# Priority of the blocks and sums of h, the place of a weight sum, and the queue place of the third HGRN pair, in a one-core hybrid encoder block

## The chip, the cores and the metric

The kernel runs on one core of one Trainium2 chip. The time is the device time of one execution in microseconds (us). The kernel before took 1408.69 us as the median of three runs (1408.69, 1410.4, 1408.69).

Five engines work beside each other, each through its own instructions in order: TensorE (PE: matmuls, PEld: weight loads), VectorE (DVE), ScalarE (ACT), GpSimd (POOL) and SyncE (SP), which here only issues loads. They wait for each other and for DMA transfers by semaphores.

## The reference

One layer of a streaming encoder for 256 tokens of width 2048, all in float32: a normed input projection, an HGRN2 recurrence with 8 heads beside a chunked attention with 16 heads, a gated merge, and a squared-ReLU MLP.

```python
def mixer_block(u, w_in, lb, hg_norm_w, rel_bias, w_branch_a, w_branch_b, w_out):
    z = u @ w_in
    hq, hf, hi, hg, aq, ak, av, gates = jnp.split(z, SPLIT_POINTS, axis=-1)
    g = lb + (1.0 - lb) * jax.nn.sigmoid(hf)
    log_g, kk = jnp.log(g), 1.0 - g
    q = jax.nn.silu(hq) * (HG_DK ** -0.5)
    o = hgrn2_scan(q, kk, hi, log_g)          # per head, S_t = diag(g_t) S_{t-1} + k_t v_t^T, o_t = S_t^T q_t
    y_a = rms_norm(o, hg_norm_w) * jax.nn.silu(hg)
    y_b = chunk_band_attention(aq, ak, av, rel_bias)
    gate_a, gate_b = jnp.split(jax.nn.sigmoid(gates), 2, axis=-1)
    merged = gate_a * (y_a @ w_branch_a) + gate_b * (y_b @ w_branch_b)
    return merged @ w_out

def reference(x, ...):
    h = x + mixer_block(rms_norm(x, norm_mix_w), ...)
    h = h + jnp.square(jax.nn.relu(rms_norm(h, norm_mlp_w) @ w_up)) @ w_down
    return rms_norm(h, norm_final_w)
```

## The kernel before

**Matmuls by split halves.** Each float32 weight tile is loaded raw (`raw`, `rawp`, `rawd`; 128x1024 elements, 512 KB), cast on ACT to a high half (`wh`, line L89) and subtracted on DVE to a low half (`wl`, L90). The activations are held as the same kind of pair (`act_x`, `act_h`, `act_m`, `S_h`). A product of a 128-row block takes three matmuls per k-tile: hi by wh (L143), hi by wl (L144), lo by wh (L145). So each weight tile of 1024 columns costs one ACT cast, one DVE subtraction and 12 matmuls of 128x512.

**Stages in order.** The projections hf and hq (transposed, `gemm_t`, L184 to L188) and hi and hg (`gemm`) with the HGRN work between them; the attention's aq, ak, av and its scores; the gates ga and gb; the branch products ba and bb; w_out (units wo0 and wo2); then four quarters of w_up (units up00, up02, up10, ...) and w_down (dn...). From the gates on, all but the branch products are `Unit`s run by `run`.

**The queue of the HGRN stage.** `later` puts (gap, function) turns into one list, `behind`. Each weight tile of a projection calls `tick` (1 per k-tile of `gemm_t`, 2 per k-tile of `gemm`), which counts the first turn's gap down and runs it when it is used up. So the small HGRN matmuls and their DVE and ACT work come between the projection's matmuls. For a pair of heads `fq(u)` gives two functions: `decay` (`hf_pair`: sigmoid, gate, `kk` L319, floor L320, Ln L322, cumulative sum L324) and `query` (`hq_pair`: factor L330, sigmoid L332, products L335 and L338). `scores` queues eight turns for a pair (diagonal ps L373, factors L384 to L406, level matmuls L417, `so` L451). `group` queues, for two pairs, four outputs (`po` matmuls L475 and L476, square L480, sum L481, `o` L486) and four finishes (`tpo` transposes L493 and their split into `act_ya`). Pairs 0 and 1 make group 0, pairs 2 and 3 group 1. `a2[1]()` and `a2[2]()` are decay and query of the third pair; in the kernel before they are called at once, while group 0's turns are still in the list.

**A unit.** `run` computes a 256x1024 piece by a Strassen-like scheme of seven products over blocks of activation sums (`S_x`, `S_m`, `S_h`: lines L680 to L686, `combos`) and of weight sums (`sums`, L817, on DVE; `sent`, L822, an accumulating DMA from POOL). Its weight blocks are A, B, C and D, each two raw tiles; p11A in a name is the weight split for product 11 with block A. Items `r1_8`, `r0_14`, ... are plain weight tiles for the k-tiles that the scheme leaves. The last plain tiles of a unit (`r1_12`, `r1_14`) are done inside the next unit, from the list `late`.

**What sets the order.** A scheduler places each instruction on its engine; priority is the program's order, moved forward by `tc.high_priority(offset=2000)`. Weight splits, weight sums and evictions of banks are so marked. The transposes of h (`tp_h`, L106), its blocks (L1013, split L89 and L90, square L1015) and its sums come as `steps` of units wo2 and up00 (`h_blocks`): h is the residual after w_out, and up00 is the first unit that reads it. Loads are issued by SP in program order when their buffer is free; the stores of h to DRAM (`hd`) and the accumulating copies go through POOL's queue.

Of the kernel before, what the change touches and what calls it, by code (L numbers as in the profile page):

```python
# [12 lines left out]
ALU = mybir.AluOpType  # L13
# [3 lines left out]
P = 128  # L17
T = 256
NM = T // P
# [17 lines left out]
def bc(ap, pos, n):  # L37

    dims = [list(d) for d in ap.ap]
    dims.insert(pos, [0, n])  # L40
    return bass.AP(tensor=ap.tensor, offset=ap.offset, ap=dims)
# [9 lines left out]
def tile_hybrid_block(  # L51
# [5 lines left out]
    nc = tc.nc  # L57
# [13 lines left out]
    wmix, wmlp = vt[:, 0:16], vt[:, 16:32]  # L71
# [16 lines left out]
    def split(hi, lo, src, copy=None):  # L88
        (copy or nc.scalar.copy)(hi, src)  # L89
        nc.vector.tensor_tensor(lo, src, hi.bitcast(F32), op=ALU.subtract)  # L90
# [68 lines left out]
    def later(*steps):  # L159
        behind.extend([n, f] for n, f in steps)  # L160
# [57 lines left out]
    for kt, n in zip(starts, steps):  # L218
# [3 lines left out]
        with tc.high_priority(offset=2000):  # L222
            for j in range(n):
                g, hi = wmix[:, kt + j:kt + j + 1], xT[c][:, a + j, 0, :]
# [116 lines left out]
    def v_chunk(g):  # L341
        acc = gemm(xT, w_in_n, C_HI + g * NC, KD, f"hi{g}")
        vs = []
        for m in range(NM):
            v = hp.tile([P, NC], F32, name=f"v{g}{m}", tag="tok", bufs=7)
            nc.scalar.activation(v, acc[:, m, :], AF.Copy, scale=rstd[:, m:m + 1])
            vs.append(v)
        return vs
# [168 lines left out]
    def scores(n, made, gap, first=None, between=()):  # L517

        sc = []
        steps = []  # L520

        def one(i):
            if not i:
                out, fs = hgrn_scores(n, made)
                sc.extend(out)
                steps.extend(fs)
            steps[i]()

        todo = [(gap if i or first is None else first, lambda i=i: one(i)) for i in range(8)]
        for at, f in between:  # L530
            todo.insert(at, (gap, f))
        later(*todo)
        return sc

    def group(g, s0, s1, vs, gws, gap, gap2):
        parts = {}

        def outputs(h0, sc, m):
            if not m:
                parts[h0] = hgrn_out(g, h0, sc, vs, gws)  # L540
            parts[h0][0][m]()

        later(*[(gap, lambda h0=h0, sc=sc, m=m: outputs(h0, sc, m)) for h0, sc in ((0, s0), (2, s1)) for m in range(NM)],
              *[(gap2, lambda h0=h0, m=m: parts[h0][1][m]()) for h0 in (0, 2) for m in range(NM)])

    ya += [new_act(f"ya{g}") for g in range(2)]
    a0, a1 = fq(0), fq(1)
# [2 lines left out]
    s0 = scores(0, a0[0], 5, 12, ((5, a1[1]), (8, a1[2])))  # L550
    vs0 = v_chunk(0)
    s1 = scores(1, a1[0], 4)
    gws0 = hg_chunk(0)
    group(0, s0, s1, vs0, gws0, 4, 3)
    a2 = fq(2)
    a2[1]()
    a2[2]()
    s2 = scores(2, a2[0], 4)
    a3 = fq(3)
    later((3, a3[1]), (3, a3[2]))  # L560
    vs1 = v_chunk(1)
    s3 = scores(3, a3[0], 4)
    gws1 = hg_chunk(1)
    group(1, s2, s3, vs1, gws1, 2, 3)
    acc_q = [gemm_t(xT, w_in_t, C_AQ + i * T, KD, f"aq0{i}") for i in range(2)]
    while behind:
        tick(9)
# [91 lines left out]
    def combos(lhs, what, home, made, blocks=None):  # L659

        a = {}

        def block(m, j):
            if blocks:
                a[m, j] = blocks[m, j]
                return
            a[m, j] = fours(token(f"a{m}{j}_{what}"))
            x = lhs[j][:, :, :, m * P:(m + 1) * P].bitcast(F32)
            nc.vector.tensor_tensor(a[m, j], x[:, :, 0, :], x[:, :, 1, :], op=ALU.add)

        def final(i, s):
            t = home.tile([P, 4, 2, P], F32R, name=f"S{i}_{what}", tag=f"S{i}", bufs=1)
            split(t[:, :, 0, :], t[:, :, 1, :], s)
            made[i] = [[t[:, k, u, :] for u in range(2)] for k in range(4)]

        def one():
            for m in range(NM):
                for j in range(2):
                    block(m, j)
            nc.vector.tensor_tensor(a[1, 1], a[1, 0], a[1, 1], op=ALU.subtract)  # L680
            final(5, a[1, 1])

        def two():
            nc.vector.tensor_tensor(a[1, 0], a[0, 0], a[1, 0], op=ALU.subtract)
            nc.vector.tensor_tensor(a[0, 0], a[1, 1], a[0, 0], op=ALU.subtract)
            nc.vector.tensor_tensor(a[0, 1], a[0, 1], a[0, 0], op=ALU.add)  # L686
            final(4, a[0, 1])

        return [one, two, lambda: final(2, a[0, 0]), lambda: final(7, a[1, 0])]
# [165 lines left out]
    def run(u, then=None):  # L855

        def q():
            if late:
                late.pop(0)()

        def item(x):
            if x and x.items:
                x.load_item()

        if not u.raw:
            u.load("A")
            u.load("B")
            u.load("C")
            u.load("D")
        for _ in range(3 - sum(type(k) is tuple for k in u.raw)):  # L870
            item(u)
        at = iter(range(99))
        u.bank("11")
        u.product("11", "A", u.block(0, 0), True)
        u.sums("A", "B")
        u.begun("21", "11")
        u.sent("B", "C")
        q()
        item(u)
        u.bank("22")  # L880
        u.product("22", "A", u.comb(5), True)
        u.sums("A", "C")
        u.begun("12", "22")
        q()
        item(u)
        u.steps = list(u.make_steps())
        u.step(next(at))
        u.product("12", "C", u.comb(4))
        u.step(next(at))
        u.product("11", "D", u.block(0, 1))  # L890
        u.sent("D", "A")
        u.step(next(at))
        u.plain(1, (8, 9))
        item(u)
        u.step(next(at))
        u.product("21", "A", u.comb(2))
        u1 = u.copy(token(f"u1_{u.what}"), "21")
        if then:
            then.load("A")
        u.step(next(at))  # L900
        u.plain(1, (10, 11))
        u.less("12", u1)
        item(u)
        u.step(next(at))
        u.product("21", "B", u.comb(7))
        u2 = u.copy(token(f"u2_{u.what}"), "21")
        if then:
            then.load("B")
            then.load("C")
        u.step(next(at))  # L910
        u.plain(0, (8, 9))
        u.less("22", u2)
        item(u)
        u.step(next(at))
        u.plain(0, (10, 11))
        item(u)
        u.step(next(at))
        u.product("21", "D", u.block(1, 1))
        if then:
            then.load("D")  # L920
        u.step(next(at))
        u.plain(0, (12, 13))
        item(u)
        u.step(next(at))
        u.plain(0, (14, 15))
        item(then)
        u.end(0)
        while u.steps:
            u.step(99)

        if u.tail:
            halves = [u.plain(1, ks, ()) for ks in LATE]
            for m in range(NM):
                for h in halves:
                    h(m)
                u.done(m, 1, u.c["12"[m] + "2"])
            return

        def rest():
            u.plain(1, LATE[1])  # L940
            u.end(1)

        late.append(lambda: u.plain(1, LATE[0]))
        late.append(rest)
# [48 lines left out]
    sp = ctx.enter_context(tc.tile_pool(name="spool", bufs=1, reuse_waits="tile"))  # L993
# [4 lines left out]
    hT = []  # L998
    Sh = {}

    hw = {}

    def h_blocks(n0):

        def one(n, m):
            if not m:
                hT.append(new_act(f"h{n}"))
            hi, lo = hT[n][:, :, 0, :], hT[n][:, :, 1, :]
            t = h1[n][m]
            tp = transpose4(t, f"h{n}{m}")  # L1010
            tmp = fours(token(f"hw_{n}_{m}"))
            hw[m, n] = tmp
            nc.vector.tensor_tensor(tmp, tp, bc(wmlp[:, 4 * n:4 * n + 4], 2, P), op=ALU.mult)  # L1013
            split(hi[:, :, m * P:(m + 1) * P], lo[:, :, m * P:(m + 1) * P], tmp)
            nc.scalar.activation(token(f"hsq_{n}_{m}"), t, AF.Square, accum_out=ssq2[:, m, n:n + 1])  # L1015

        def factor():
            ssum2 = small.tile([P, NM], F32, name="ssum2", tag="ssum")
            nc.vector.tensor_reduce(ssum2, ssq2, axis=AX.X, op=ALU.add)
            rsqrt(rstd2, ssum2, D, NM)  # L1020

        return [(n if n0 else 99, lambda n=n, m=m: one(n, m)) for n in (n0, n0 + 1) for m in range(NM)] + [
            (99, f, 6) for f in ([factor] if n0 else combos(hT, "h", sp, Sh, hw))]

    rstd2 = const.tile([P, NM], F32, name="rstd2")

# [15 lines left out]
    for qd in range(NQ):  # L1042
# [64 lines left out]
        for n0 in (0, 2):  # L1107
            units.append(Unit(lambda uT=uT: uT, lambda Su=Su: Su, w_down, n0 * NC, f"dn{qd}{n0}",
                              lambda m, n, acc, n0=n0, out_of=out_of: out_of(m, n0 + n, acc), kt0=qd * KD,
# [49 lines left out]
```

## Time and profile before

| what | value |
|---|---|
| median of three runs | 1408.69 us |
| profiled execution | 1406.51 us, span 1404.8 us |
| TensorE clock granted, mean | 0.998 |
| PE busy | 1386.3 us (99%) |
| DVE busy | 1118.1 us (80%) |
| ACT busy | 909.6 us (65%) |
| POOL busy | 137.3 us (10%) |
| read from HBM, written | 271.67 MB, 10.49 MB |

The profile is of one execution. A row of the timeline gives start, duration, engine, line, operation, output and inputs, and in square brackets the idle time before it and who ended it. A row of the waits gives who waited, for whom, the total in us, the count and the longest. Records overlap on PE since matmuls are pipelined: 128x512 matmuls start 0.227 us apart while each record lasts 0.39.

### The profile page before, as it was taken

Reading aid. Unit: us, or ns where it says so; the run is one execution under the profiler, and the core shown is the slowest. Engines: PE = TensorE matmul, PEld = TensorE weight load, DVE = VectorE, ACT = ScalarE, POOL = GpSimd, SP = SyncE. Lnnn points to the kernel's source line nnn. Section 1 sums busy time; section 2 is a strip of 40 time slices with the busy share of each in tenths; the row PEclk is TensorE's granted clock in tenths of the full one; section 3 lists DMA queues with packets and bytes.
Section 4 is the critical chain, followed back from the end, with each engine's and each line's share of the span. In section 5 each row is a group of like instructions: output and inputs, shape, how many; then the busy total and the mean of one; then the engine's idle time right before and its main releaser. Section 6 shows DMA issues by size and latency. Waiting matters only on the chain.

```text
span 1404.8 us, 18581 instructions
## 1 busy us (share of the span) xinstructions
PE 1386.3 (99%) x6562; PEld 1148.6 (82%) x6562; DVE 1118.1 (80%) x1406; ACT 909.6 (65%) x1170; POOL 137.3 (10%) x220
## 2 busy tenths in 40 slices
PE   9999999999999999999999999999999999999997
PEld 8888888878787888888877888888888888888885
DVE  7898987675758785698988977789877897878885
ACT  6775644464656664346767876678666876668764
POOL 3000001010000000001210001100011001110200
PEclk9999999999999999999999999999999999999999
DMA  9654455655578987658988889988899888998883
GB/s 330 230 174 151 151 165 159 192 171 173 157 234 263 272 249 231 191 171 274 265 265 252 244 267 273 269 268 242 251 292 303 243 224 258 280 302 257 263 246 117
DMA packets 122925, 327.42 MB, mean 233 GB/s; under 512 B 10944, under 2 KB 11712, under 8 KB 122448
## 3 DMA queue, kind: packets, MB, share of 16 engines
q1 hardware_dynamic: 103264, 264.80, 55.1%
q0 software_dynamic: 18416, 59.84, 21.5%
q10 hardware_dynamic: 1152, 1.60, 0.4%
q8 instruction: 51, 0.84, 0.2%
q14 instruction: 42, 0.34, 0.1%
HBM read 271.67 MB, written 10.49 MB: 201 GB/s over the span
## 4 chain that ended last, share of the span: by engine, by line
PE 93%; DVE 2%; DMA 2%; ACT 1%; issue 1%; POOL 0%; POOLq 0%; SPq 0%; ACTq 0%; DVEq 0%
PE acc_ak L185 2%; PE acc_aq L185 2%; PE acc_hq L185 2%; DMA raw_hf<-in_w_in_t_dram 1%; PE acc_hf L185 1%; PE tp_u L106 1%; PE acc_ga L144 1%; PE acc_ga L145 1%; PE acc_bb L143 1%; PE acc_bb L145 1%; PE acc_hg L145 1%; PE acc_hg L144 1%; PE acc_ba L145 1%; PE acc_av L143 1%; PE acc_ba L143 1%; PE acc_hg L143 1%
## 5 line engine op out<-in xcount | busy, mean ns | idle before, releaser
L185 PE MATMUL acc_aq<-act_x,wh_aq 128*128 128x512 f32 x128 | 46.6, 400 | 0.0
L185 PE MATMUL acc_hf<-act_x,wh_hf 128*128 128x512 f32 x128 | 45.9, 397 | 0.2 <-DVE f L193 0.2
L185 PE MATMUL acc_hq<-act_x,wh_hq 128*128 128x512 f32 x128 | 45.9, 395 | 0.0
L185 PE MATMUL acc_ak<-act_x,wh_ak 128*128 128x512 f32 x128 | 44.8, 396 | 0.0
L184 PE MATMUL acc_aq<-act_x,wl_aq 128*128 128x256 f32 x120 | 35.2, 294 | 0.0
L90 DVE TENSOR_TENSOR wl_ga<-raw_ga,wh_ga 128x1024 fp32r<-128x1024 f32 x16 | 19.6, 1226 | 19.5 <-ACT wh_ga L89 19.4
L184 PE MATMUL acc_hq<-act_x,wl_hq 128*128 128x256 f32 x120 | 34.2, 285 | 0.0
L184 PE MATMUL acc_hf<-act_x,wl_hf 128*128 128x256 f32 x120 | 34.1, 284 | 0.0
L90 DVE TENSOR_TENSOR wl_av<-raw_av,wh_av 128x1024 fp32r<-128x1024 f32 x16 | 19.6, 1224 | 17.6 <-ACT wh_av L89 17.6
L184 PE MATMUL acc_ak<-act_x,wl_ak 128*128 128x256 f32 x120 | 33.5, 279 | 0.0
L89 ACT CAST wh_bb<-raw_bb 128x1024 fp32r<-128x1024 f32 x16 | 16.9, 1054 | 23.3 <-PE acc_ba L145 17.7
L90 DVE TENSOR_TENSOR wl_bb<-raw_bb,wh_bb 128x1024 fp32r<-128x1024 f32 x16 | 19.6, 1223 | 14.9 <-ACT wh_bb L89 14.8
L89 ACT CAST wh_av<-raw_av 128x1024 fp32r<-128x1024 f32 x16 | 16.8, 1053 | 22.0 <-PE acc_av L145 12.4
L89 ACT CAST wh_ba<-raw_ba 128x1024 fp32r<-128x1024 f32 x16 | 16.8, 1053 | 20.6 <-PE acc_bb L145 13.2
L90 DVE TENSOR_TENSOR wl_ba<-raw_ba,wh_ba 128x1024 fp32r<-128x1024 f32 x16 | 19.6, 1224 | 12.2 <-ACT wh_ba L89 12.2
L89 ACT CAST wh_aq<-raw_aq 128x1024 fp32r<-128x1024 f32 x16 | 16.8, 1048 | 18.3 <-PE acc_hg L145 9.3
L185 PEld LDWEIGHTS acc_hf<-act_x,wh_hf 128*128 128x128 f32 x128 | 24.1, 188 | 5.4 <-DVE f L193 0.6
L90 DVE TENSOR_TENSOR wl_aq<-raw_aq,wh_aq 128x1024 fp32r<-128x1024 f32 x16 | 19.6, 1223 | 11.2 <-ACT wh_aq L89 11.2
L185 PEld LDWEIGHTS acc_aq<-act_x,wh_aq 128*128 128x128 f32 x128 | 24.1, 188 | 5.3 <-issue 0.7
L185 PEld LDWEIGHTS acc_ak<-act_x,wh_ak 128*128 128x128 f32 x128 | 23.9, 188 | 5.4
L89 ACT CAST wh_ga<-raw_ga 128x1024 fp32r<-128x1024 f32 x16 | 16.8, 1051 | 17.6 <-PE acc_ga L145 9.2
L185 PEld LDWEIGHTS acc_hq<-act_x,wh_hq 128*128 128x128 f32 x128 | 24.0, 188 | 5.0
(1805 smaller groups left out, 5245.4 us busy)
## 6 DMA issues: line engine op xcount, KB each, us to landing
raw_hi<-in_w_in_n_dram SPq DMA_DIRECT2D x16, 512.0 KB, 4.6
raw_hg<-in_w_in_n_dram SPq DMA_DIRECT2D x16, 512.0 KB, 3.7
raw_aq<-in_w_in_t_dram SPq DMA_DIRECT2D x16, 512.0 KB, 3.9
raw_ak<-in_w_in_t_dram SPq DMA_DIRECT2D x16, 512.0 KB, 4.0
raw_av<-in_w_in_n_dram SPq DMA_DIRECT2D x16, 512.0 KB, 4.3
raw_ga<-in_w_in_t_dram SPq DMA_DIRECT2D x16, 512.0 KB, 3.7
raw_ba<-in_w_branch_a_dram SPq DMA_DIRECT2D x16, 512.0 KB, 4.5
raw_bb<-in_w_branch_b_dram SPq DMA_DIRECT2D x16, 512.0 KB, 4.7
```

The source lines that it names most:

```text
L89: (copy or nc.scalar.copy)(hi, src)
L90: nc.vector.tensor_tensor(lo, src, hi.bitcast(F32), op=ALU.subtract)
L106: nc.tensor.transpose(tp[:, j, :], src[:, j * P:(j + 1) * P], ident)
L143: nc.tensor.matmul(acc, hi, wh, start=first, stop=False, skip_group_check=True)
L144: nc.tensor.matmul(acc, hi, wl, start=False, stop=False, skip_group_check=True)
L145: nc.tensor.matmul(acc, lo, wh, start=False, stop=last, skip_group_check=True)
L184: nc.tensor.matmul(acc[:, cb, 0:T], wl[:, c], r[:, 0, :], start=False, stop=False)
L185: nc.tensor.matmul(acc[:, cb, :], wh[:, c], r.rearrange("p u t -> p (u t)"), start=kt == 0, stop=kt == nkt - 1)
```

## The change

Three edits.

1. In `h_blocks`, the product of the transposed h with the norm's gains and its split, and all later steps (`combos` for the first half, the sum of squares for the second), run under `high_priority(offset=2000)`, the level of the weight splits.
2. In `run`, `u.sums("A", "C")` moves from behind product 22 to behind product 12 with C: in program order C's splits now stand before the sum A+C.
3. `group` no longer queues its finishes but returns them. For group 0, the third pair's decay and query are queued, three ticks each, behind the four outputs and in front of the finishes; before, they were run at once. For group 1 the finishes are queued right behind its outputs, as before. All turns after the third pair's decay and query come 6 ticks later in the list.

```diff
-        later(*[(gap, lambda h0=h0, sc=sc, m=m: outputs(h0, sc, m)) for h0, sc in ((0, s0), (2, s1)) for m in range(NM)],
-              *[(gap2, lambda h0=h0, m=m: parts[h0][1][m]()) for h0 in (0, 2) for m in range(NM)])
+        later(*[(gap, lambda h0=h0, sc=sc, m=m: outputs(h0, sc, m)) for h0, sc in ((0, s0), (2, s1)) for m in range(NM)])
+        return [(gap2, lambda h0=h0, m=m: parts[h0][1][m]()) for h0 in (0, 2) for m in range(NM)]
...
-    group(0, s0, s1, vs0, gws0, 4, 3)
+    turns0 = group(0, s0, s1, vs0, gws0, 4, 3)
     a2 = fq(2)
-    a2[1]()
-    a2[2]()
+    later((3, a2[1]), (3, a2[2]), *turns0)
...
-    group(1, s2, s3, vs1, gws1, 2, 3)
+    later(*group(1, s2, s3, vs1, gws1, 2, 3))
...
         u.product("22", "A", u.comb(5), True)
-        u.sums("A", "C")
...
         u.product("12", "C", u.comb(4))
+        u.sums("A", "C")
...
-            nc.vector.tensor_tensor(tmp, tp, bc(wmlp[:, 4 * n:4 * n + 4], 2, P), op=ALU.mult)
-            split(hi[:, :, m * P:(m + 1) * P], lo[:, :, m * P:(m + 1) * P], tmp)
+            with tc.high_priority(offset=2000):
+                nc.vector.tensor_tensor(tmp, tp, bc(wmlp[:, 4 * n:4 * n + 4], 2, P), op=ALU.mult)
+                split(hi[:, :, m * P:(m + 1) * P], lo[:, :, m * P:(m + 1) * P], tmp)
...
+        def soon(f):
+            with tc.high_priority(offset=2000):
+                f()
+
         return [(n if n0 else 99, lambda n=n, m=m: one(n, m)) for n in (n0, n0 + 1) for m in range(NM)] + [
-            (99, f, 6) for f in ([factor] if n0 else combos(hT, "h", sp, Sh, hw))]
+            (99, lambda f=f: soon(f), 6) for f in ([factor] if n0 else combos(hT, "h", sp, Sh, hw))]
```

## The prediction

> **What bounds the kernel now.** I read the page's busy shares first, then TensorE's waits, then the rows of PE, DVE and ACT around each wait. The profiled execution took 1406.51 us (span 1404.8), 2.2 us under the median of 1408.69; sums below are made against it.
>
> ```profile
> PE 1386.3 (99%) x6562; PEld 1148.6 (82%) x6562; DVE 1118.1 (80%) x1406; ACT 909.6 (65%) x1170; POOL 137.3 (10%) x220
> ```
>
> ```profile
> PE acc_up00c L145 <- DVE S_h L90: 1.6, 1, 1.6
> PE acc_up00c L143 <- ACT wh_up00r L89: 1.2, 1, 1.2
> PE po L476 <- DVE o L486: 1.1, 1, 1.1
> ...
> PE acc_ga2c L144 <- DVE wl_ga2p11D L90: 1.0, 1, 1.0
> ```
>
> TensorE is the bound, and its waits on others are a handful of single events. A gain can only come from removing them. Three places matter: the first `up` unit (720 to 740), the HGRN outputs (142 and 224) and `ga2` (426):
>
> ```profile
> 142.28 0.68 PE L476 MATMUL po<-v,sd 128*128 128x128 f32 x4 [1.12 <-DVE o L486]
> ```
> ```profile
> 224.74 0.46 PE L475 MATMUL po<-v,so 128*128 128x128 f32 x2 [0.32 <-DVE o L486]
> ```
> ```profile
> 720.00:740.00 20.00, 16.57 (x73) 12.09 (x72) 19.87 (x21) 12.60 (x18) 2.84 (x4) 1.00 1.01 291
> ```
>
> The last row (columns: PE, PEld, DVE, ACT, POOL, clock, DMA share, GB/s) shows the worst stretch: PE works 16.57 of 20 us at full clock, DVE 19.87. In this stretch DVE is the limit. These are the PE rows that I count from there:
>
> ```profile
> 710.25 0.39 PE L143 MATMUL acc_wo2c<-wh_wo2r,act_m 128*128 128x512 f32 x1
> 710.47 0.39 PE L144 MATMUL acc_wo2c<-wl_wo2r,act_m 128*128 128x512 f32 x1
> ...
> 712.97 0.39 PE L143 MATMUL acc_up00c<-wh_up00p11A,act_h 128*128 128x512 f32 x1
> ...
> 715.91 0.39 PE L144 MATMUL acc_wo2c<-wl_wo2r,act_m 128*128 128x512 f32 x1
> ...
> 741.17 0.60 PE L106 MATMUL tp_h<-ident,h 128*128 128x128 f32 x4
> 741.53 0.48 PE L144 MATMUL acc_up00c<-wl_up00r,act_h 128*128 128x512 f32 x1
> ...
> 752.87 0.39 PE L143 MATMUL acc_up00c<-wh_up00p21D,act_h 128*128 128x512 f32 x1
> ```
>
> A weight group is 12 matmuls in 712.97 − 710.25 = 2.72 us. From 710.25 to the first matmul of p21D at 752.87 PE runs 13 groups and four `tp_h` transposes (0.36 each by 741.53 − 741.17): 35.4 + 1.4 = 36.8 us of work in 42.6. So **5.8 us are lost there**.
>
> **The change, part 1: blocks and sums of h at high priority.** Why DVE is late there:
>
> ```profile
> 706.88 1.23 DVE L90 TENSOR_TENSOR wl_wo2r<-rawp_wo2r,wh_wo2r 128x1024 fp32r<-128x1024 f32 x1 [3.68 <-ACT wh_wo2r L89]
> ...
> 716.24 1.28 DVE L754 TENSOR_TENSOR h<-acc_wo2c,h 128x512 f32<-128x512 f32 x2
> 717.43 2.35 DVE L90 TENSOR_TENSOR wl_up00p22A<-raw_up00A,wh_up00p22A 128x1024 fp32r<-128x1024 f32 x2
> ...
> 729.98 1.89 DVE L90 TENSOR_TENSOR S_h<-hw,S_h 128x512 fp32r<-128x512 f32 x3
> ```
> ```profile
> 705.80 1.05 ACT L89 CAST wh_wo2r<-rawp_wo2r 128x1024 fp32r<-128x1024 f32 x1 [4.65 <-DMA rawp_wo2r<-in_w_out_dram]
> 706.75 0.61 ACT L89 CAST S_h<-hw 128x512 fp32r<-128x512 f32 x1
> 707.27 1.05 ACT L89 CAST wh_up00p11A<-raw_up00A 128x1024 fp32r<-128x1024 f32 x1
> ```
>
> A load ends at 705.80 and holds both ACT and DVE; the S_h splits that PE needs are done only at 729.98. Starts are 2.35 − 1.22 = 1.13 us apart for a 1024-wide DVE operation and 1.28 − 0.68 = 0.60 for a 512-wide one; on ACT 0.95 and 0.52. In the new instruction order the `combos` arithmetic and the three S_h splits stand ahead of the split of wo2's last first-half weight (wl_wo2r at 706.88). The arithmetic (L680 to L685) fits into DVE's idle 3.68 us. The splits don't, because their casts queue behind the same late cast: ACT casts S7 at 706.75, S2 at 707.27, p11A at 707.79, S4 at 708.74 to 709.36. DVE then runs S2, S7, S4 from 707.95 to 710.03 and wl_wo2r from 710.03 to 711.25. PE wants it at 710.47: a **new wait of 0.85**. Behind it DVE runs p11A twice, a sum, an `h`, a sum, an `h`: 1.13 × 5 + 0.60 × 2 = 6.85, so the next wo2 split runs 716.88 to 718.10. PE wants it at 715.91 + 0.85 = 716.76: a **new wait of 1.4**. From there each split that I place comes 0.4 to 1 us before its group (p11D 1.0, up00r 0.4 to 0.65), and the S_h and wh_up00r waits have no cause left: S_h is done 20 us early, and Square (L1015) stands behind the cast it blocked at 738. New loss 0.85 + 1.4, and 0.1 for each restart (the matmul at 741.53, behind a pause, takes 0.48 and not 0.39): 2.45 against 5.8, a gain of 3.3. Slacks of 0.4 us by hand can fail by some tenths; I take **−3.0**, and as bounds −4.5 (the two new waits half as long, other losses gone) and 0 (one of S_h's 1.6 and wh_up00r's 1.2 back, and small waits at each group).
>
> Moved with it: loads whose buffer a later split frees. SP issues the next `up` weight when wl_wo2r has been read:
>
> ```profile
> 708.13 14.31 SPq L724 DMA_DIRECT2D rawp_up00r<-in_w_up_dram  x3
> ```
> ```profile
> rawp_wo2r<-in_w_out_dram SPq DMA_DIRECT2D x4, 512.0 KB, 9.4
> ```
>
> It goes out about 3.2 us later (711.3). With the 9.4 us to landing that the wo2 loads of this stretch took (690 to 720) it lands by 720.7. PE comes to it five groups and three transposes behind the second new wait: 718.15 + 13.6 + 1.1 = 732.9, and cast and split take 2.2 of that. Hidden by some 10 us. On POOL's queue the stores of h move ahead of the accumulating copies into D; D's rows are needed by the p21D splits after 745, so I cost that at nothing (half a megabyte at 291 GB/s is 1.8 us).
>
> Prices here rest on DVE's start distance. The Trainium skill, page "VectorE: DVE Perf Modes", section "The DRAIN you can't avoid", says a drain of about the operation's duration less 266 ns follows each DVE operation before the next starts. Read as time added, 1.22 would cost 2.18 and the second new wait would grow by 6.2 us, to a total of 1410.6. The rows at 717.43 show 1.13 instead, so this case decides against it, and I give it 1 in 100.
>
> **Part 2: the sum A+C behind C's splits.** The wait it could remove is at 426:
>
> ```profile
> 424.08 1.22 DVE L90 TENSOR_TENSOR wl_ga2p12C<-raw_ga2C,wh_ga2p12C 128x1024 fp32r<-128x1024 f32 x1
> 425.21 2.35 DVE L90 TENSOR_TENSOR wl_ga2p11D<-rawd_ga2D,wh_ga2p11D 128x1024 fp32r<-128x1024 f32 x2
> ```
>
> In the new order ga2's instructions stand exactly as before, since the scheduler had placed the sum when its inputs were ready; units gb0, wo2 and dn32 swap one sum with one split where PE doesn't wait. So **0** (bounds −1.1, the wait at 426 gone, and +0.5, about half of a 1.13 us operation ahead of a split with little slack).
>
> **Part 3: third pair's decay and query behind the HGRN outputs.** Ahead of the `o` that PE waits for at 142.28 stand, on ACT, three table loads (first and last shown), and on DVE the scan and its products:
>
> ```profile
> 132.09 1.28 ACT L322 ACT_TABLE_LOAD   x1
> ...
> 138.43 1.28 ACT L385 ACT_TABLE_LOAD   x1
> ```
> ```profile
> 134.05 1.23 DVE L324 TENSOR_TENSOR_SCAN b<-reset,lg 128x512 f32<-128x512 f32 x1 [0.34 <-ACT lg L322]
> ...
> 141.53 0.61 DVE L486 SCALAR_TENSOR_TENSOR o<-po,ro,gw 128x128 f32<-128x128 f32 x2 [0.82 <-POOL ro L96]
> ```
>
> All of it moves behind the last output, so the first `o` comes near 137.5 instead of 141.5 and the PE wait of 1.12 goes, with 0.2 of restarts (1.3). The turns behind shift by 6 ticks, a tick being one weight tile (4 matmuls of acc_hq). The wait at 224.74 (0.49 with its restart) goes too: `gw` then leads the output by 24 more matmuls. Against this: the moved work meets the finishes; DVE is full from 149.6 to 158, and the fourth transpose of `o` is due at 158.2 when its buffer comes free: 0 to 0.5, I take 0.2. The last finish of pair two now stands 4 matmuls before acc_ak starts, where 28 stood. Its PE bank needs the eviction of acc_aq:
>
> ```profile
> 236.50 0.68 DVE L193 TENSOR_TENSOR aq00T<-acc_aq,aq00T 128x512 f32<-128x512 f32 x1
> ```
>
> By its steps (cast on ACT, 0.68 on DVE, behind a split of 1.22 that may stand in front of it) I put it 0.3 behind PE, an estimate, with 0 (no split in front) and 1 (a whole one) as ends. Sum −1.3 − 0.5 + 0.2 + 0.3 = **−1.3** (−1.8 with no new wait; +0.4 with both new waits at their ends, 1.5, and half of the 142 wait kept).
>
> **Sum.** −3.0 + 0 − 1.3 = −4.3: profile 1406.5 → 1402.2, median 1408.7 → **1404.4**.
>
> **Rivals.**
> 1. *The h work keeps DVE's backlog and only moves the wait.* DVE is busy 19.87 of 20 us already, and its new start (707.95) is 1.07 us later than 706.88. If p11D and up00r each miss by 1 to 1.5 us, the 3.0 are gone: 1408.7 − 1.3 = **1407.4**, no change. Against it: DVE idles again after 741, and none of the displaced splits is due at once.
> 2. *Slower: h tiles as a ring.* At high priority each of four h tiles makes a trip PE (tp_h), DVE (hw), ACT (cast), DVE (split), and DVE, in order, holds weight splits behind it. A wait on a late split of this kind cost 1.8 us of PE at S_h (1.6 and the restarts). Four of them cost 7.1, against gains of 4.3: **1411.5**. It decides when each trip costs more than 1.1 (no gain) or 1.8 (slower by over 0.2%). For it: DVE's strict order; against: tp_h ends 0.5 us and more before its hw is at the head of DVE.
> 3. *Part 3 gives nothing, part 1 all*: new waits at tpo and acc_ak eat the 1.3: **1405.7**.
> 4. *The sum's move also frees ga2*: 1.1 more, **1403.3**. Against it: the unchanged order.
>
> **Chances.** Forecast 0.44, rival 1 0.23, rival 2 0.14, rival 3 0.13, rival 4 0.05, the drain 0.01. What a measurement can tell from no change is 0.2%, 2.8 us (1405.9). Faster: 0.44 + 0.05 and 0.09 of rival 3's 0.13 = 0.58; same: 0.23 + 0.04 + 0.01 = 0.28; slower: 0.14. The forecast's own range is 1402.2 to 1406.5. The whole one goes from 1401.5 (part 1 at −4.5, part 3 at −1.8 would be 1402.4, and ga2 a part of 1.1) up to 1411.0, leaving out most of rival 2.
>
> **What would show it.** Right: no PE wait at 142 and 224, none on S_h or wh_up00r; waits of about 0.85 near 711 and 1.4 near 718 on wl_wo2r; p21D's first matmul about 4.3 us earlier than 752.87 (1.3 of it from part 3); ga2's 1.0 unchanged. Wrong: new waits on wl_up00p11D, act_h or wl_up00r; wl_hi or acc_ak waits above 1 us at 155 to 165 and 245 to 250.

## The result and the profile after

The changed kernel takes 1403.92 us, median of 7 runs, against 1408.17 us for the kernel before in the same comparison: a ratio of 0.9969, 95% interval 0.9958 to 0.9981, so 2.7 to 5.9 us less. The forecast was 4.3 less and 1404.4. Its profiled execution took 1403.92 us as well, with a span of 1402.2; the profiled execution before (1406.51, span 1404.8) was shorter than any of its kernel's seven runs, so the two traces differ by 2.6 us only.

The page's first part and the waits of TensorE, changed kernel:

```profile
PE 1385.6 (99%) x6562; PEld 1149.9 (82%) x6562; DVE 1116.7 (80%) x1406; ACT 909.4 (65%) x1170; POOL 138.6 (10%) x220
```
```profile
PE acc_wo2c L144 <- DVE wl_wo2r L90: 2.1, 2, 1.1
...
PE acc_ga2c L144 <- DVE wl_ga2p11D L90: 1.0, 1, 1.0
PE acc_ak L185 <- DVE aq00T L193: 0.7, 1, 0.7
...
PE tpo L493 <- DVE act_ya L90: 0.4, 1, 0.4
```

The waits on `S_h`, on `wh_up00r` and on `o` are gone. Two on wl_wo2r have come for the first two, and one each at `acc_ak` and `tpo` for the third. ga2's 1.0 stands as it was.

The same stretch as before (columns: busy time of PE, PEld, DVE, ACT, POOL; clock; DMA share; GB/s), and where PE waits in it:

```profile
700.00:720.00 20.00, 17.85 (x77) 14.07 (x77) 17.59 (x23) 11.77 (x16) 2.86 (x4) 1.00 0.74 249
720.00:740.00 20.00, 20.00 (x97) 16.55 (x96) 20.00 (x24) 16.10 (x24) 2.83 (x4) 1.00 1.01 275
```
```profile
670.69 0.39 PE L143 MATMUL acc_wo2c<-wh_wo2p11A,act_m 128*128 128x512 f32 x1
...
712.13 0.50 PE L144 MATMUL acc_wo2c<-wl_wo2r,act_m 128*128 128x512 f32 x1 [1.01 <-DVE wl_wo2r L90]
...
719.00 0.50 PE L144 MATMUL acc_wo2c<-wl_wo2r,act_m 128*128 128x512 f32 x1 [1.14 <-DVE wl_wo2r L90]
...
750.74 0.39 PE L143 MATMUL acc_up00c<-wh_up00p21D,act_h 128*128 128x512 f32 x1
...
758.90 0.39 PE L143 MATMUL acc_up02c<-wh_up02p11A,act_h 128*128 128x512 f32 x1
```

From 720 to 740 PE is busy all the time, where it was busy 16.57 of 20; it pays between 700 and 720 instead. From wo2's first matmul (670.69) to up02's first (758.90) the stretch takes 88.21 us. Before it took 90.77 (670.26 to 761.03):

```profile
670.26 0.39 PE L143 MATMUL acc_wo2c<-wh_wo2p11A,act_m 128*128 128x512 f32 x1
...
761.03 0.39 PE L143 MATMUL acc_up02c<-wh_up02p11A,act_h 128*128 128x512 f32 x1
```

That is 2.56 less, and DVE and ACT took the order that was forecast:

```profile
708.77 1.30 DVE L90 TENSOR_TENSOR S_h<-hw,S_h 128x512 fp32r<-128x512 f32 x2 [2.23 <-ACT S_h L89]
710.25 0.69 DVE L90 TENSOR_TENSOR S_h<-hw,S_h 128x512 fp32r<-128x512 f32 x1 [0.18 <-ACT S_h L89]
710.86 1.22 DVE L90 TENSOR_TENSOR wl_wo2r<-rawp_wo2r,wh_wo2r 128x1024 fp32r<-128x1024 f32 x1
...
717.73 1.22 DVE L90 TENSOR_TENSOR wl_wo2r<-rawp_wo2r,wh_wo2r 128x1024 fp32r<-128x1024 f32 x1
```
```profile
706.65 1.05 ACT L89 CAST wh_wo2r<-rawp_wo2r 128x1024 fp32r<-128x1024 f32 x1 [3.60 <-DMA rawp_wo2r<-in_w_out_dram]
707.61 1.14 ACT L89 CAST S_h<-hw 128x512 fp32r<-128x512 f32 x2
```

Three S_h splits, then the late wl_wo2r, and 6.87 us later (717.73 − 710.86) the next one.

In the HGRN stage the two new waits, and what DVE does at the first:

```profile
159.18 0.44 PE L493 MATMUL tpo<-ident,o 128*128 128x128 f32 x2 [0.45 <-DVE act_ya L90]
```
```profile
240.07 0.50 PE L185 MATMUL acc_ak<-act_x,wh_ak 128*128 128x512 f32 x1 [0.66 <-DVE aq00T L193]
```
```profile
157.56 1.23 DVE L90 TENSOR_TENSOR wl_hi<-raw_hi,wh_hi 128x1024 fp32r<-128x1024 f32 x1
158.70 0.76 DVE L90 TENSOR_TENSOR act_ya<-tpo,act_ya 128x256 fp32r<-128x256 f32 x2
```

By the starts of the matmuls (the distance to the matmul before, less the usual 0.227) they cost 0.62 and 0.83. The split that frees the transposes' buffer stands behind a weight split on DVE. From hg's first matmul to av's first, which holds all HGRN work that moved, the traces give 184.29 us before (78.04 to 262.33) and 184.00 after (78.76 to 262.76): **0.3 gained, not 1.3**.

### The profile page after: what moved, and what is told of

Same layout as the page of the kernel before. It is cut to its first block, busy times and chain, and to the rows that moved or that the text cites. A ratio compares the mean times of both kernels' runs of the same rounds, so it can differ in the third digit from the quotient of the medians.

```text
span 1402.2 us, 18580 instructions
## 1 busy us (share of the span) xinstructions
PE 1385.6 (99%) x6562; PEld 1149.9 (82%) x6562; DVE 1116.7 (80%) x1406; ACT 909.4 (65%) x1170; POOL 138.6 (10%) x220
## 4 chain that ended last, share of the span: by engine, by line
PE 93%; DVE 2%; DMA 2%; issue 1%; ACT 1%; POOL 0%; ACTq 0%; POOLq 0%; DVEq 0%
PE acc_ak L185 2%; PE acc_aq L185 2%; PE acc_hf L185 1%; PE ps L417 1%; PE acc_hq L185 1%; PE acc_ga L144 1%; PE tp_u L106 1%; PE acc_ga L145 1%; PE acc_hg L143 1%; PE acc_hg L144 1%; PE acc_bb L143 1%; PE acc_ba L145 1%; PE acc_av L144 1%; PE acc_hg L145 1%; PE acc_ba L143 1%; PE acc_bb L145 1%
```

## The experiments

Times and ratios are against the kernel before, run on the same chip beside it. Two lengths are read in each trace: the *stretch* (wo2's first matmul to up02's first) and *hg to av*.

**Part 1 alone.** Edit: only `h_blocks` as changed.

> Part 1 alone: blocks and sums of h at high priority, turns and the sum A+C as before. Theory (the h work carries the gain): no PE wait on S_h or wh_up00r, two waits of 1.0 to 1.2 on wl_wo2r near 711 and 718, p21D's first matmul 2.6 us earlier counted from the first w_out matmul, time 2.6 under before (ratio 0.998). Rival (the gain is made in the HGRN turns, the h work only moves its wait): p21D within 0.5 us of before, time within 0.8 of before.

Measured: 1405.44 against 1409.7, ratio 0.9974 (0.9965 to 0.9983). So it is by far the largest part of the gain, and the rival's time (within 0.8 of before) is out. But the profiled execution, at 1406.58 one of the slower ones of the eleven, showed a stretch of 90.59, hardly shorter than before, and p21D only 0.18 earlier, with one wait in place of two:

```profile
PE acc_wo2c L144 <- DVE wl_wo2r L90: 2.9, 1, 2.9
```
```profile
708.89 1.05 ACT L89 CAST wh_wo2r<-rawp_wo2r 128x1024 fp32r<-128x1024 f32 x1 [3.76 <-DMA rawp_wo2r<-in_w_out_dram]
```

Neither theory had such a stretch together with such a time. The cast of the late load starts 38.14 us after wo2's first matmul here (708.89 − 670.75), and 35.96 in the changed kernel (706.65 − 670.69): the load landed 2.2 us later in this execution. That made the landing itself a suspect, and the table after the next runs follows it. Behind the long wait the granted clock fell as well (the last three columns are clock, DMA share and GB/s):

```profile
700.00:720.00 20.00, 17.11 (x69) 13.65 (x68) 15.41 (x21) 9.54 (x13) 1.70 (x3) 0.91 0.75 271
```

From 715.9 to 718.5 the matmuls start 0.427 us apart in place of 0.227. A clock of 0.91 over 20 us is 1.8 us of TensorE's work; the second of the two waits is gone in its place.

**Part 3 alone.** Edit: only the queue of the third pair as changed.

> Part 3 alone: third pair's decay and query behind the first group's outputs. Theory (two new waits take back most of what the removed ones give): waits at 142 and 224 gone (1.3 and 0.5), new ones on act_ya at tpo (0.4 to 0.6) and on aq00T at acc_ak (0.7 to 0.8), net 0.3 from the first hg matmul to the first av matmul, time 0.3 under before. Rival (the size forecast): net 1.3. Second rival (what the medians leave beside 2.6 for part 1): 1.7.

Measured: 1409.25 against 1409.7, ratio 1.0001 (0.9992 to 1.001). Hg to av: 184.03, 0.26 less than before, with the 0.4 at `tpo` and the 0.7 at `acc_ak` in its waits. The theory holds; 1.3 and 1.7 are out.

**Part 2 alone.** Edit: only the line `u.sums("A", "C")` moved.

> Part 2 alone: the sum A+C behind C's splits. Theory: DVE's order in ga2 is unchanged, PE's 1.0 on wl_ga2p11D stays, time within 0.4 of before; at most a short wait near 1356 (0.27) goes. Rival: the sum frees p11D's splits in some units, 1.1 to 1.5 under before.

Measured: 1408.21 against 1409.7, ratio 0.9994 (0.9985 to 1.0003): no change that can be told from none. ga2's wait:

```profile
PE acc_ga2c L144 <- DVE wl_ga2p11D L90: 1.0, 1, 1.0
```

The short wait near 1356 was gone here, but it was gone with part 3 alone too, so it isn't the sum's.

**S2 and S7 later.** Edit, on the changed kernel:

```diff
-        def soon(f):
-            with tc.high_priority(offset=2000):
+        def soon(f, offset=2000):
+            with tc.high_priority(offset=offset):
                 f()
...
-            (99, lambda f=f: soon(f), 6) for f in (...)]
+            (99, lambda f=f, i=i: soon(f, 2000 if i < 2 else 1920), 6) for i, f in enumerate(...)]
```

> The changed kernel, but the splits of S2 and S7 at an offset of 1920 in place of 2000, so that they stand behind wo2's last splits. Theory (the two new waits come from three splits put ahead of wl_wo2r): both waits under 0.3; DVE is still the limit of the stretch, so 0.5 to 1.5 come back as waits on wl_up00p11D or wl_up00r; 1 to 2 us under the changed kernel. Rival (the late load and its cast set the waits): at least 0.8 of each stays, time as the changed kernel's.

Measured: 1403.49 against 1409.7, ratio 0.9956 (0.9944 to 0.9968). Both waits on wl_wo2r are gone, and one on p11D has come:

```profile
PE acc_up00c L144 <- DVE wl_up00p11D L90: 1.1, 1, 1.1
```

So the order of the splits made the two waits, as the theory had it, and DVE's backlog gives most of them back (1.35 by the starts). The stretch is 87.19 with the cast at 35.43, 0.5 better than the changed kernel's at equal landing (51.76 against 52.27, below). The 1 to 2 us that were expected under the changed kernel did not come.

**The landing.** "Cast" is the start of the late load's cast after wo2's first matmul. In each of these traces it follows the landing of that load by 0.10 us, so it stands for the landing.

| kernel | order of DVE in the stretch | cast | stretch | stretch − cast |
|---|---|---|---|---|
| before | before | 35.54 | 90.77 | 55.23 |
| part 2 alone | before, one sum moved | 35.68 | 90.90 | 55.22 |
| part 3 alone | before | 37.44 | 92.67 | 55.23 |
| changed | changed | 35.96 | 88.21 | 52.25 |
| part 1 alone | as changed but for two sums | 38.14 | 90.59 | 52.45 |
| finishes, last group (below) | changed | 36.15 | 88.43 | 52.28 |
| finishes, both groups (below) | changed | 36.66 | 88.94 | 52.28 |
| S2 and S7 later | changed, two splits later | 35.43 | 87.19 | 51.76 |

The last column is the same to 0.2 us within each order. A microsecond of later landing costs a microsecond, in either order; and the changed order is worth 55.23 − 52.27 = **2.96 us** at equal landing. The 2.56 seen between the two profiles is this less 0.42 of later landing. Part 1 alone gives 2.78 by this measure; whether the 0.2 between is the two sums that part 2 moves in this stretch or that execution's late landing isn't shown.

**Sums of h alone.** Edit: only `soon` for the later steps, blocks of h as before.

> Half of part 1: only the sums of h (combos and their splits S4, S2, S7) at high priority; blocks of h and their splits as before. Theory (S_h's late splits were the largest wait; the blocks' late splits hold the square and wh_up00r at 738): the 1.8 of S_h goes, 2.2 to 2.4 of new waits on wl_wo2r come, the wait on wh_up00r stays or moves to act_h: gain of 1.0 to 2.0 against before. Rival (blocks do nothing of their own): as with both, 2.6.

Measured: 1407.74 against 1408.47, ratio 0.9992 (0.9983 to 1.0). Stretch 91.43 with the cast at 36.85: 54.58, or 0.65 better than before at equal landing, less than expected, and the time can hardly be told from that before. Waits:

```profile
PE acc_wo2c L144 <- DVE wl_wo2r L90: 2.9, 2, 1.8
...
PE acc_up00c L143 <- ACT act_h L89: 0.8, 1, 0.8
...
PE tp_h L106 <- DVE hw L1013: 0.4, 1, 0.4
```

**Blocks of h alone.** Edit: only the first `high_priority` block, later steps as before.

> Other half of part 1: only the blocks of h (product with the gains, and split) at high priority, sums as before. Theory: S_h's splits now stand behind all four blocks on DVE (after p21B's first split), so PE waits for S_h longer than before: 3 to 8 us slower than before. Rival (PE's order moves with them, the scheduler puts the matmuls on S_h later): within 1 us of before.

Measured: 1412.43 against 1408.47, ratio 1.0027 (1.0019 to 1.0036): slower. Stretch 94.49 with the cast at 36.08: 58.41, 3.2 worse at equal landing.

```profile
737.56 1.89 DVE L90 TENSOR_TENSOR S_h<-hw,S_h 128x512 fp32r<-128x512 f32 x3
```
```profile
738.30 0.79 PE L145 MATMUL acc_up00c<-wh_up00p12C,S_h 128*128 128x512 f32 x1 [3.03 <-DVE S_h L90]
...
739.31 0.63 PE L144 MATMUL acc_up00c<-wl_up00p12C,S_h 128*128 128x512 f32 x1
739.74 0.63 PE L145 MATMUL acc_up00c<-wh_up00p12C,S_h 128*128 128x512 f32 x1
```
```profile
738.00:740.00 2.00, 1.70 (x4) 1.42 (x5) 1.69 (x5) 0.00 (x0) 0.19 (x1) 0.50 1.02 382
```

The blocks pass S_h's splits, which come at 737.56 instead of 729.98. TensorE's wait for them is 1.5 us longer than before by the starts (3.31 against 1.77). Behind it matmuls again start 0.43 us apart at a clock of 0.50: in the four windows of 2 us from 736 to 744 the clock is 0.97, 0.50, 0.68 and 1.00, which is 1.7 us lost. The two make the 3.2; the wait on wh_up00r (1.2) is gone, and waits on act_h (0.6 and 0.4) have come about in its place. The median lost 4.0. Ten of the eleven runs had a mean clock of 0.995 or 0.996, the profiled one 0.997 and the runs beside it 0.996 to 0.998, so the clock may have cost more in the others; no trace shows that.

So the halves don't add: −0.65 and +3.2 alone, −2.78 together (part 1 alone). Each half alone leaves the other half's work behind on a full DVE.

**Last group's finishes sooner.** Edit, on the changed kernel: `group(1, s2, s3, vs1, gws1, 2, 2)`.

> The changed kernel, but the last group's finishes 2 ticks apart, not 3: 16 matmuls more between the last tpo and acc_ak. Theory (aq00T waits for the last finish, and acc_ak for aq00T): the 0.7 to 0.8 at acc_ak goes, nothing else moves: 0.6 to 0.9 under the changed kernel. Rival (aq00T's eviction is late because DVE is): the wait stays above 0.5.

Measured: 1403.95 against 1408.47, ratio 0.9962 (0.9948 to 0.9976); the changed kernel's own median was 1403.92, in another comparison. The expected 0.6 to 0.9 did not come. The wait at `acc_ak` is gone, so the late finish did cause it; but hg to av is 184.05, as in the changed kernel (184.00), because a wait of the same size stands before a finish:

```profile
234.51 0.44 PE L493 MATMUL tpo<-ident,o 128*128 128x128 f32 x2 [0.76 <-DVE act_ya L90]
```

**Both groups' finishes.** Edit: in addition `group(0, s0, s1, vs0, gws0, 4, 4)`.

> As the run before, and the first group's finishes 4 ticks apart, not 3. Theory (the wait at tpo is the DVE burst of the moved decay meeting the finishes, each tpo needing the buffer that act_ya frees): with 4 ticks the 0.6 at 158 goes too; 1.2 to 1.5 under the changed kernel. Rival (DVE is behind by a fixed amount from there on): the wait moves to wl_hi or ps, nothing more gained than with the last group's finishes alone.

Measured: 1403.51 against 1408.47, ratio 0.9963 (0.995 to 0.9975), not the 1.2 to 1.5 under the changed kernel that were expected. The wait at 158 is gone, as expected, but hg to av is 184.26: the later turns meet the end of the stage.

```profile
237.41 0.44 PE L493 MATMUL tpo<-ident,o 128*128 128x128 f32 x2 [0.74 <-DVE act_ya L90]
240.40 0.50 PE L185 MATMUL acc_ak<-act_x,wh_ak 128*128 128x512 f32 x1 [0.25 <-DVE aq00T L193]
```

In these two runs moving turns only moved the wait, and no gain can be told from none.

**Splits and sum later.** Edit: S2 and S7 later as above, and the sum behind D's splits:

```diff
         u.product("12", "C", u.comb(4))
-        u.sums("A", "C")
         u.step(next(at))
         u.product("11", "D", u.block(0, 1))
+        u.sums("A", "C")
         u.sent("D", "A")
```

> The changed kernel with S2's and S7's splits at offset 1920 and, besides, the sum A+C behind p11D's splits in place of behind C's. Theory (with the two wl_wo2r waits gone, DVE's backlog in front of p11D, two sums of 1.13 each, sets the 1.35 on wl_up00p11D): that wait falls under 0.3, the stretch from wo2's first matmul to up02's first is 1.0 to 1.4 shorter than with the later splits alone at the same landing of the late load; ga2's 1.0 stays, since its order is the same. Rival (the wait only moves to up00r and p21A): stretch within 0.4.

Measured: 1402.91 against 1408.13, ratio 0.9959 (0.9944 to 0.9974). Stretch 86.97, cast 35.21: 51.76, exactly as without the sum. The rival was right: the wait went from p11D to up00r.

```profile
PE acc_up00c L144 <- DVE wl_up00r L90: 1.1, 1, 1.1
```

**x behind the wo2 load.** Edit, on the changed kernel; DVE's order stays the same:

```diff
-        with tc.high_priority(offset=2000):
-            nc.gpsimd.dma_start(t, x[m * P:(m + 1) * P, n * NC:(n + 1) * NC])
+        if n < 2:
+            with tc.high_priority(offset=2000):
+                nc.gpsimd.dma_start(t, x[m * P:(m + 1) * P, n * NC:(n + 1) * NC])
+        else:
+            nc.sync.dma_start(t, x[m * P:(m + 1) * P, n * NC:(n + 1) * NC])
```

> The changed kernel, but the four 256 KB loads of x for the second half of h go through SP's queue behind wo2's last first-half load, where POOL issued them beside it; DVE's order is the same. Theory (the landing of that load sets when ACT and DVE go on, and so the length of the stretch, about 1 us for 1 us): its cast comes 0.5 to 1.5 earlier than 35.4 us after wo2's first matmul, and the stretch shrinks by as much: below 87.7. Rival (the order of DVE alone sets it): the stretch stays at 88.2 whatever the landing.

Measured: 1402.3 against 1408.13, ratio 0.9954 (0.9938 to 0.997). Cast 34.48, stretch 86.77: 52.29, on the line of the table. With the splits of the changed order untouched, the earlier landing alone took the first of the two waits away; 1.0 on the second is left. The four moved loads, which also lose their raised priority, are issued 5.1 to 8.5 us after the late one here; in the changed kernel POOL issued them from 2.8 before it to 3.4 after it.

**All of it.** Edit: the two runs before in one.

> Both of the runs before in one. Theory: the gains add until PE's own work of the stretch is all that is left: stretch 85 to 86, time 1401 to 1402 (2 to 3 under the changed kernel). Rival (DVE is full from the late load on, so they don't add): as the better of the two.

Measured: 1401.78 against 1408.13, ratio 0.9953 (0.9939 to 0.9967): the fastest kernel here, 2.1 under the changed one by their medians, with intervals that still overlap. Its waits and the stretch:

```profile
PE ps_warm L81 <- DVE warm L79: 1.1, 1, 1.1
PE acc_ga2c L144 <- DVE wl_ga2p11D L90: 1.0, 1, 1.0
PE acc_ak L185 <- DVE aq00T L193: 0.7, 1, 0.7
PE ps L373 <- DVE q L338: 0.5, 1, 0.5
PE acc_hq L188 <- DVE wl_hq L90: 0.5, 1, 0.5
PE tpo L493 <- DVE act_ya L90: 0.4, 1, 0.4
```
```profile
700.00:720.00 20.00, 20.00 (x90) 16.57 (x89) 20.00 (x24) 13.43 (x16) 2.81 (x4) 1.00 0.90 291
720.00:740.00 20.00, 20.00 (x98) 16.53 (x97) 19.88 (x25) 15.85 (x25) 2.83 (x4) 1.00 0.90 251
```

No wait is left in the stretch: 85.43, with the cast at 32.07, 0.7 after the landing: the load no longer sets it. PE is full, and DVE all but full.

**All of it without part 3.** Edit: the run before with the third pair's turns as in the kernel before.

> The run with both in one (later splits and sum, x behind the wo2 load), but with the third pair's decay and query as before (part 3 undone). Theory (part 3 is worth 0.3): from the first hg matmul to the first av matmul 184.3 us in place of 184.1, waits on o at 142 and 224 back, time within 1.0 of 1401.8. Rival (part 3 is worth the 1.3 of the forecast or more): 1403 or more, and 185 us from hg to av.

Measured: 1403.29 against 1409.14, ratio 0.9961 (0.9948 to 0.9975): 1.5 above the run with part 3 by the medians, which the intervals don't tell apart. The stretch is again 85.43, though the cast came at 32.37: here PE's own work sets it. Hg to av is 184.92, 0.87 more than with part 3 (184.05). That is more than the theory's 0.3; the time and the 184.92 come out at the rival's 1403 and 185, though 0.87 is less than its 1.3. Beside the waits on `o` it shows one that the profile before lacks:

```profile
PE po L476 <- DVE o L486: 1.1, 1, 1.1
...
PE po L475 <- ACT f L192: 0.4, 1, 0.4
```

The trace of part 2 alone has it too, and 184.93. Of the six profiles with the old order of the turns four lie at 184.28 to 184.32 and two at 184.92 and 184.93; with the new order six lie at 184.00 to 184.05 (one of them with the last group's finishes moved), one at 184.26 with both groups' finishes moved, and one at 183.59. So part 3 is worth about 0.3 beside four of the six profiles with the old order and 0.9 beside two. Whether the new order rules the wait on `f` out, or eight profiles happened to miss it, is not shown.

## Why the prediction was right, and where it was not

**Part 1 (−3.0 forecast): right.** At equal landing it gave 2.96 with part 2 beside it and 2.78 alone. The order of the steps is in the rows: S2 and S7, S4, wl_wo2r, and the next wo2 split 6.87 us later (6.85 forecast). The new waits were 1.17 and 1.30 by the starts, against 0.85 and 1.4; the first is longer because the load landed 0.42 later than in the profile that the forecast was worked out from. None came on p11D or up00r, whose slacks had been put at 0.4 to 1.0, and S_h and wh_up00r have no wait. The later up00r load and the stores of h cost PE no wait. The forecast's p21D, 4.3 earlier than 752.87, came at 750.74, 2.1 earlier: the 2.56 of the stretch and the 0.29 of part 3, less 0.72 by which this execution's first hg matmul was later.

**Part 2 (0): right.** The unchanged order in ga2 kept its 1.0, and alone the move showed no change. Rival 4 is out.

**Part 3 (−1.3): wrong by about 1.0.** The step that failed is the one that sized the two new waits: 0.2 at `tpo` (0 to 0.5) and 0.3 at `acc_ak` (0 to 1). They measured 0.62, outside its range, and 0.83, with another 0.11 of restart. Both mechanisms were named, and the removed waits, 1.3 and 0.5, went as forecast; 1.77 − 1.56 leaves the 0.2 to 0.3 seen. At `tpo` the forecast named no weight split in front of `act_ya`; in the trace one of 1.23 stands there (wl_hi at 157.56). Rival 3, that part 3 gives nothing and part 1 all, describes the traces better than the forecast's own case.

**The sum.** 2.96 and 0.3 make 3.3, inside the measured 2.7 to 5.9 but 1.0 short of the 4.25 between the medians. Between the two traces the account closes: 2.56 in the stretch, 0.29 in the HGRN stage and 0.46 behind up02's first matmul (643.77 against 643.31, of which 0.27 is a short wait near 1356), less the 0.72 of later start, make the 2.6 between the spans. For the medians three things can fill part of the rest: the wait on `f` at `po`, 0.6 in some executions with the old turns; the mean landing of the late load, which may differ between the kernels; and the granted clock, which was 0.996 or 0.997 in 12 of the 27 runs of the kernel before beside the first four experiments (1410.3 in the mean, against 1408.7 at 0.998). One profile each can't show how much, and it stays open. So the time came out at the forecast in part by luck: one of its terms was 1.0 too large, and whether something of that size was left out, or the median only stands that far from the sum, the interval doesn't say.

**Rivals 1 and 2.** The backlog did not eat the gain in the full change; with only half of part 1 it ate most of it (sums alone 0.65) or more (blocks alone, 3.2 lost). Slower by a ring of h tiles didn't happen: tp_h, hw and act_h have no wait with both halves. What made blocks alone slower is S_h behind the blocks and the clock behind that wait; the ring's kind of wait, on act_h, was 1.0 in all there, no more than the 1.2 on wh_up00r that it replaced.

**The rule on drains.** With a pause behind each DVE operation, as the drain's rival priced it, the second new wait would have been 7.6 us. It was 1.30, and seven operations took 6.87 us. The Trainium skill, page "VectorE: DVE Perf Modes", section "The DRAIN you can't avoid", has a drain of about the operation's duration less 266 ns behind each; read as added time, the rule doesn't hold here.

## What to carry to other kernels

Where one engine is full in a stretch, look at all the work that a common consumer needs before raising the priority of some of it: of part 1's two halves one alone gave 0.65 us in the stretch and the other alone cost 3.2, where both together gave 2.8 to 3.0. A wait removed by moving turns in a queue has to be followed to where the turns land: here two of them took back most of it, and moving the turns again only moved the wait. A long wait of TensorE can cost more than its length, so look at the granted clock behind it. When stretches of two profiles differ, measure them from the moment their late load lands before crediting the order.

## What was not expected of the hardware

The landing of one 512 KB load decided the length of a stretch of 90 us in either order, and its cast came from 35.2 to 38.1 us after the stretch's start with the order of the loads untouched. The spread comes mostly from the issue of the load (24.3 to 27.6 us after the start); from issue to landing it took 10.3 to 11.6. The issue follows an earlier transfer. SP issues its loads in order, and one ahead of the late load, the second raw_up00B, waits for the second accumulating copy in POOL's queue. In all fourteen traces it goes out 0.06 or 0.07 us after that copy has landed, and the late load 2.1 to 2.9 us after the landing. SP's waits for the two copies, first the changed kernel, then part 1 alone (who waited, for whom, total, count, longest):

```profile
SPq L723 <- DMA rawd_wo2D<-raw_wo2A: 6.3, 2, 4.3
```
```profile
SPq L724 <- DMA rawd_wo2D<-raw_wo2A: 9.0, 2, 5.4
```

With part 1 alone the second copy landed 3.2 us later than in the changed kernel (25.23 against 22.07 after the start). Why the copy's landing varies stays open.

Issuing four 256 KB loads behind the late load rather than beside it brought its landing forward. The late load alone, first in the changed kernel, then with x behind it, then with all edits (KB, us to landing):

```profile
rawp_wo2r<-in_w_out_dram SPq DMA_DIRECT2D x1, 512.0 KB, 11.3
```
```profile
rawp_wo2r<-in_w_out_dram SPq DMA_DIRECT2D x1, 512.0 KB, 9.7
```
```profile
rawp_wo2r<-in_w_out_dram SPq DMA_DIRECT2D x1, 512.0 KB, 7.2
```

In the run with all edits but part 3 it took 8.0. So the three traces with the loads of x behind lie at 7.2 to 9.7, below all eleven others. Why two of them are shorter than the third stays open.

The granted clock fell in the middle of two traces only, to 0.50, each time behind a wait of TensorE of about 3 us (2.89 with part 1 alone, 3.03 with blocks alone), and it cost some 1.7 us more each time. Behind the next longest wait of these traces, 1.8 with sums alone, it stayed at 1.00.

The start varies as well: hg's first matmul, ahead of which none of these kernels differ, came between 77.97 and 80.84 us in the fourteen profiles.
